# Differential attention: the scores of a head as three products over 64 rows, its two halves in turn

## The chip, the cores and the metric

One core of one Trainium2 chip. The metric is device microseconds of one launch; lower is better. The core has five engines with instruction streams of their own: PE (TensorE, the matrix products), DVE (VectorE), ACT (ScalarE), POOL (GpSimd) and SP (SyncE, which here only issues DMA transfers). They wait for each other by semaphores. Matrix products read SBUF and write PSUM; DVE and ACT read the products from PSUM.

## What is computed

Two hybrid layers (an RWKV mixer, a short convolution and differential attention side by side, then an output projection), with an attention layer, two feed-forward layers and a recurrent layer around and behind them. The change is in differential attention. A head has width 128, made of two halves of 64; each half has a softmax of its own, and the second is subtracted from the first:

```
q_l, k_l = rope(heads(q)), rope(heads(k))            # heads: (token, head, half j of 2, 64)
s    = einsum('bqhjd,bkhjd->bhjqk', q, k) * 64**-0.5
p    = softmax(s)
attn = p[:, :, 0] - lam * p[:, :, 1]
o    = einsum('bhqk,bkhe->bqhe', attn, v)
o    = rms_norm(o) * (1 - lam_init) * silu(z)
```

There are 512 tokens of the sequence and 256 of a context. Layer 0 has 4 heads and six query blocks of 128: blocks 0 to 3 look at all 768 keys, blocks 4 and 5 at 256. Layer 1 has 4 heads and four query blocks, all against 768 keys.

## The kernel before

Operands are kept in two parts, high and low (type fp32r), and a product is the sum hi·hi + hi·lo + lo·hi. The q and k of each head lie split in DRAM, 128 rows (two halves of 64) by tokens.

`attn_phase` runs an order written out by hand for PE, DVE and ACT; each executes its instructions in the order of the program. POOL and SP are placed by a scheduler. The loop goes over the units of all heads, where a unit is one head and one query block (24 in layer 0, 16 in layer 1). Iteration i issues, in this order:

- `scores(i, 0)`, `scores(i, 1)`: for each half j, matrix products into a PSUM tile `s` (tag `s2`, two buffers of 128x1024, one for each half). Then for that half DVE takes the row maximum (`mx`, L1177), and ACT the exponential with its sum (`p`, L1179).
- finishing work of a head, where one is due (transposes at L1251, product with the gate; the reciprocal root).
- `combine(i-1)` on DVE: `rc` (L1189, L1190) and `A = p0 + rc*p1` (L1192).
- `transpose(i-2)`: A is turned by PE in blocks of 128 (L1204) into the tile `ax`; ACT casts the high part `ath` (L1207) and DVE subtracts for the low part `atl` (L1208).
- `values(i-3)`, for every second unit: attn by v on PE (L1219), evicted twice by ACT (`osq`, `osb`).
- one step of a modulation stream that belongs to the next stages (layer 0 in every iteration, layer 1 in every second): a weight is loaded, split by ACT (`whi`, L295) and POOL (`wlo`, L298), and multiplied on PE (L817, L818); now and then L837 puts a finished row into `ax`.

`load(h)` brings the operands of a head: that of head 0 ahead of the loop, the others when the second unit of the head before is built. The stacked form is what the first matrix product of a key range needs: `qs[j]` holds q's high part of half j in 64 rows and its low part in the other 64; `kd[j]` holds k's high part of half j twice. So L1173 makes hi·hi + lo·hi in one product over 128 rows, and L1174 adds hi·lo over 64 rows from `kl`. Key ranges are columns 0 to 512 and 512 to 768 of `s`.

In the later attention layer ("attn2"), a pair of heads has the same three products over 64 rows already, from unstacked operands (L1842); the first head's three are issued ahead of the second's.

Of the kernel before, what the change touches and what calls it, by code (L numbers as in the profile page):

```python
# [19 lines left out]
P = 128  # L20
# [20 lines left out]
T = TL + TC  # L41
# [172 lines left out]
class Kern:  # L214
# [881 lines left out]
    def attn_phase(self, l, es):  # L1096
        nc = self.nc
        self.wpool = WP[1]
        last = l == DEPTH - 1
        D_ = self.D_  # L1100
# [9 lines left out]
        n = TL if last else T  # L1110
        with ExitStack() as e2:
            p2 = self.pool("ps2", space=PSUM, es=e2)
            pa = self.pool("paa", space=PSUM, es=e2)
            self.pm, self.nmm = pa, 1
            ap = self.pool("at", es=e2)
# [14 lines left out]
            nc.vector.tensor_scalar(out=sg, in0=self.pc(f"subln{l}"), scalar1=0.5 * (1.0 - lam0), scalar2=None, op0=ALU.mult)  # L1130
            def load(h):


                H = dict(h=h)
                lo64, hi64 = slice(0, 64), slice(64, P)
                (qh, ql), (kh, kl) = D_[f"q{h}"], D_[f"k{h}"]
                H["kl"] = self.t(ap, [P, T], "kl", 2, F32R)
                H["qs"], H["kd"] = [], []
                for j, r in enumerate((lo64, hi64)):
                    a, b = self.t(ap, [P, T], f"qs{j}", 2, F32R), self.t(ap, [P, T], f"kd{j}", 2, F32R)  # L1140
                    for i, o in enumerate((lo64, hi64)):
                        nc.sync.dma_start(out=a[o, 0:n].bitcast(F32), in_=(qh, ql)[i ^ j][r, 0:n])
                        nc.sync.dma_start(out=b[o, :].bitcast(F32), in_=kh[r, :])
                    H["qs"].append(a)
                    H["kd"].append(b)
                nc.sync.dma_start(out=H["kl"].bitcast(F32), in_=kl)
                H["v"] = self.t(ap, [P, 6, 128], "vhi", 2, F32R), self.t(ap, [P, 6, 128], "vlo", 2, F32R)
                for i, v in enumerate(H["v"]):
                    nc.sync.dma_start(out=v.bitcast(F32), in_=D_["v"][i][:, :, h * 128:h * 128 + 128].rearrange("b p c -> p b c"))
                H["z"] = self.t(ap, [P, T], "z", 2)  # L1150
                nc.sync.dma_start(out=H["z"][:, 0:n], in_=D_[f"z{h}"][:, 0:n])
                H["osb"], H["osq"] = self.t(ap, [P, T], "osb", 2), self.t(ap, [P, T], "osq", 1)
                H["mx"], H["sm"] = self.t(ap, [P, 6, 2], "mx", 2), self.t(ap, [P, 6, 2], "sm", 2)
                for c, nm in {0: ((2, "yc0"), (3, "yc1")), 1: ((0, "yr0"), (1, "yr1"))}.get(h, ()):
                    for i in range(2):
                        nc.sync.dma_start(out=self.yh[c][i][:, 0:n].bitcast(F32), in_=D_[nm][i][:, 0:n])
                return H
# [1 line left out]

            first = lambda qp: 0 if qp < 2 else 512  # L1160

            def scores(u, j):

                H, qp, qi = u["H"], u["qp"], u["qi"]
                k0 = first(qp)
                nk = T - k0
                q = slice(qp * 256 + qi * 128, qp * 256 + qi * 128 + 128)
                r = slice(j * 64, j * 64 + 64)
                s = self.t(p2, [P, 1024], "s2", 2)[:, 0:nk]
                qs, kd = H["qs"][j], H["kd"][j]  # L1170
                for a, b in ((0, min(nk, 512)), (512, nk)):
                    if b > a:
                        nc.tensor.matmul(s[:, a:b], lhsT=qs[:, q], rhs=kd[:, k0 + a:k0 + b], start=True, stop=False)  # L1173
                        nc.tensor.matmul(s[:, a:b], lhsT=qs[r, q], rhs=H["kl"][r, k0 + a:k0 + b], start=False, stop=True)  # L1174
                c = qp * 2 + qi
                mx, sm = (H[x][:, c, j:j + 1] for x in ("mx", "sm"))
                nc.vector.tensor_reduce(out=mx, in_=s, axis=AX.X, op=ALU.max, negate=True)  # L1177
                e = self.t(ap, [P, T], f"p{j}", 2)
                nc.scalar.activation(e[:, 0:nk], s, AF.Exp, bias=mx, accum_out=sm)  # L1179
                u["p"].append(e[:, 0:nk])  # L1180

            def combine(u):

# [50 lines left out]
            def gains(p_):  # L1234

                H, a, b = (p_[x] for x in "Hab")
                cols = self.rsqrt_step(*p_["rs"])
                nb = (b - a) // P
                p_["dg"] = self.t(ap, [P, 6, P], "dg", 1)
                e1, e2 = (nc.vector if p_["quick"] else nc.gpsimd for i in range(2))  # L1240
                e1.tensor_copy(out=p_["dg"][:, 0:nb, :], in_=cols.unsqueeze(2).broadcast_to([P, nb, P]))
                e2.tensor_tensor(out=H["osb"][:, a:b], in0=H["osb"][:, a:b], in1=H["z"][:, a:b], op=ALU.mult)

            def finish(p_):
                H, t0, t1 = (p_[x] for x in "Hab")
# [13 lines left out]
            with tc_manual(self.tc, MS):  # L1259
                heads = [load(0)]  # L1260
                us, due, parts = [], {}, {}
                at = lambda i: us[i] if 0 <= i < N else None
                for i in range(N + 7):
                    if i < N:
                        h, c = divmod(i, nq)
                        if c == 1 and h < 3:
                            heads.append(load(h + 1))
                        us.append(dict(H=heads[h], qp=c // 2, qi=c % 2, p=[], last=c == nq - 1))
                    u, a, t, v = at(i), at(i - 1), at(i - 2), at(i - 3)
                    for j in range(2):  # L1270
                        if u:
                            scores(u, j)
                    if i - 2 in due:
                        finish(parts[i - 2])
                    if i - 1 in due:
                        gains(parts[i - 1])
                    if a:
                        combine(a)
                    for j in range(2):
                        if t:  # L1280
                            transpose(t, 4 * j)
                    if v and v["qi"]:
# [427 lines left out]
    def attn2(self):  # L1710


        nc = self.nc
# [6 lines left out]
        ap = self.pool("a2", es=e2)  # L1720
        hi, lo = self.h
# [93 lines left out]
        hs = (slice(0, 64), slice(64, 128))  # L1815
# [19 lines left out]

        def scores(u):
            (qh, ql), (kh, kl) = get(QK, (0, u["hp"]), 2)
            u["ps"] = []
            for h in hs:
                ps = self.t(self.pm, [P, 512], "z0", 2)  # L1840
                for i, (x, y) in enumerate(((qh, kh), (qh, kl), (ql, kh))):
                    nc.tensor.matmul(ps[:, 0:u["nk"]], lhsT=x[h, u["q"]], rhs=y[h, 0:u["nk"]], start=i == 0, stop=i == 2)  # L1842
                u["ps"].append(ps)

        def soft(u):
            u["s"] = []
# [87 lines left out]
        def get(table, key, n):  # L1934
            while len(table.get(key, ())) < n:
                fill(1)
            return table[key]
# [22 lines left out]
        with tc_manual(self.tc, SM):  # L1960
            us = []
            fill(CF[3])
            bias = {0: biases(0)}
            P_ = {}
            for i in range(18):
                u = None
                if i < 16:
# [3 lines left out]
                    u = dict(hp=hp, qb=qb, nk=(qb + 1) * 128, q=slice(qb * 128, qb * 128 + 128), bias=bias[hp], p=P_[hp])  # L1971
# [16 lines left out]
                if i == 6:  # L1988
# [7 lines left out]
                    t = self.t(a3, [P, 128], "tr")  # L1996
# [206 lines left out]
```

## Time and profile before

| | |
|---|---|
| runs | 2801.47, 2799.72, 2792.19 us; median 2799.72 |
| profiled execution | 2795.74 us, of which the span of the core is 2794.0 |
| busy over the span | PE 90%, PEld (weight loads) 74%, DVE 55%, ACT 37%, POOL 27% |
| mean granted clock of TensorE | 0.938 |
| layer 0's attention loop | 585.8 to 742 us of the span, and the last units behind it |
| layer 1's attention loop | 1305.9 to about 1418 us |

PE's busy time is modelled from pipelined instructions, so the distance between two starts (the pitch) says more than a duration. The granted clock is 1.00 at 2.4 GHz and 0.50 at 1.2 GHz. Two rows that print alike and overlap stand as one row with x2.

### The profile page before, as it was taken

What the parts mean: (1) busy time and instruction counts of PE and PEld (TensorE: products, weight loads), DVE (VectorE), ACT (ScalarE), POOL (GpSimd) and SP (SyncE); (2) the same over time, 40 slices, a digit from 0 to 9 for tenths busy, and PEclk for the clock granted to TensorE, in tenths of its full rate; (3) what the DMA queues carried; (4) which work ended last, traced back from release to release, by engine and by line L of the source; (5) the groups of instructions that cost most, each with busy time, mean ns of one, the idle gap of its engine ahead of it and who ended that gap; (6) DMA issues with size and microseconds to landing.
All of it is one profiled execution on the core that took longest, in us unless ns stands there. A gap on an engine that the chain in (4) does not pass through costs nothing.

```text
span 2794.0 us, 42466 instructions
## 1 busy us (share of the span) xinstructions
PE 2522.0 (90%) x16698; PEld 2074.8 (74%) x16698; DVE 1530.4 (55%) x2949; ACT 1030.2 (37%) x1946; POOL 743.1 (27%) x635
## 2 busy tenths in 40 slices
PE   4989998979888989998988998899999987999997
PEld 2767776845687766766668877788888876988886
DVE  7266665236644477643756666564432676644423
ACT  4232222235534322322554456543222455433221
POOL 2311113314453222221223245331101353411101
PEclk8999999978899998998899999999999998999999
DMA  5332334475331333336531211212233222232232
GB/s 209 116 111 72 84 91 148 140 208 153 123 104 59 124 97 101 93 103 202 160 106 42 72 54 38 76 61 91 94 91 97 73 68 77 77 104 91 91 96 77
DMA packets 174935, 284.85 MB, mean 102 GB/s; under 512 B 53776, under 2 KB 110992, under 8 KB 174736
## 3 DMA queue, kind: packets, MB, share of 16 engines
q1 hardware_dynamic: 174736, 282.15, 32.6%
q8 instruction: 131, 2.15, 0.3%
q14 instruction: 68, 0.56, 0.1%
HBM read 235.68 MB, written 46.40 MB: 101 GB/s over the span
## 4 chain that ended last, share of the span: by engine, by line
PE 35%; DVE 8%; ACT 5%; DMA 2%; POOL 2%; issue 2%; SPq 0%; POOLq 0%; ACTq 0%; DVEq 0%
PE mm L1483 6%; PE mm L1481 6%; PE mm L1484 6%; PE mm L1520 5%; PE mm L322 4%; PE mm L1587 2%; PE s L1174 1%; ACT whi L295 1%; PE s L1173 1%; PE z L1823 1%; DMA wraw<-in_fg_dram 1%; DVE wl L304 1%; DVE wlo L298 1%; DVE w L1859 1%; PE po L1219 1%
## 5 line engine op out<-in xcount | busy, mean ns | idle before, releaser
L295 ACT CAST whi<-wraw 128x1024 fp32r<-128x1024 f32 (+2 forms) x311 | 318.0, 1026 | 648.2 <-PE mm L1483 281.9
L298 POOL TENSOR_TENSOR wlo<-wraw,whi 128x1024 fp32r<-128x1024 f32 (+1 forms) x122 | 291.4, 2391 | 703.7 <-ACT whi L295 675.3
L1483 PEld LDWEIGHTS mm<-hlo,whi 128*128 128x128 f32 x1632 | 311.4, 191 | 74.0
L322 PE MATMUL mm<-hhi,whi 128*128 128x512 f32 (+1 forms) x992 | 330.0, 364 | 17.1 <-DVE sz L925 6.0
L1481 PE MATMUL mm<-hhi,whi 128*128 128x512 f32 x816 | 329.1, 403 | 9.5 <-ACT whi L295 9.3
L1483 PE MATMUL mm<-hlo,whi 128*128 128x256 f32 x1632 | 332.2, 286 | 0.0
L1484 PE MATMUL mm<-hhi,wlo 128*128 128x512 f32 x816 | 325.7, 400 | 6.4 <-POOL wlo L298 6.4
L298 DVE TENSOR_TENSOR wlo<-wraw,whi 128x1024 fp32r<-128x1024 f32 (+1 forms) x189 | 234.4, 1244 | 175.8 <-ACT whi L295 172.9
L322 PE MATMUL mm<-hlo,whi 128*128 128x512 f32 (+1 forms) x992 | 321.8, 360 | 0.2 <-POOL hlo L863 0.2
L322 PE MATMUL mm<-hhi,wlo 128*128 128x512 f32 (+1 forms) x992 | 319.2, 358 | 0.0
L322 PEld LDWEIGHTS mm<-hhi,whi 128*128 128x128 f32 x992 | 186.3, 201 | 49.0 <-DVE sz L925 6.9
L322 PEld LDWEIGHTS mm<-hlo,whi 128*128 128x128 f32 x992 | 183.7, 201 | 23.9 <-issue 3.6
L322 PEld LDWEIGHTS mm<-hhi,wlo 128*128 128x128 f32 x992 | 182.9, 201 | 24.3 <-issue 2.1
L1481 PEld LDWEIGHTS mm<-hhi,whi 128*128 128x128 f32 x816 | 155.3, 190 | 14.5 <-ACT whi L295 11.5
L1484 PEld LDWEIGHTS mm<-hhi,wlo 128*128 128x128 f32 x816 | 158.6, 195 | 7.5 <-POOL wlo L298 7.5
L2054 POOL TENSOR_TENSOR g<-g,rsb 128x512 f32<-128x512 f32 x44 | 57.5, 1307 | 397.4 <-DVE g L2053 397.4
L1177 DVE TENSOR_REDUCE mx<-s 128x1 f32<-128x768 f32 (+1 forms) x80 | 67.4, 849 | 78.7 <-PE s L1174 78.3
L1520 PE MATMUL mm<-yhi,whi 128*128 128x256 f32 (+1 forms) x280 | 93.3, 335 | 12.4 <-ACT whi L295 10.5
L1549 POOL TENSOR_TENSOR acc<-acc,sq 128x256 f32<-128x256 f32 x48 | 51.2, 1071 | 195.1 <-ACT sq L1547 195.1
L1179 ACT ACTIVATE p<-s,mx 128x768 f32<-128x768 f32 (+1 forms) x80 | 65.1, 815 | 102.3 <-DVE mx L1177 88.3
L2056 DVE SCALAR_TENSOR_TENSOR th<-mm,g 128x512 f32<-128x512 f32 x44 | 30.4, 690 | 115.7 <-PE mm L1484 108.8
L1520 PE MATMUL mm<-yhi,wlo 128*128 128x256 f32 (+1 forms) x280 | 91.6, 328 | 0.0
(432 smaller groups left out, 5797.0 us busy)
## 6 DMA issues: line engine op xcount, KB each, us to landing
wraw<-in_win_dram SPq DMA_DIRECT2D x76, 512.0 KB, 3.6
wraw<-in_modw_dram SPq DMA_DIRECT2D x48, 512.0 KB, 4.5
wraw<-in_fg_dram SPq DMA_DIRECT2D x44, 512.0 KB, 3.3
wraw<-in_fu_dram SPq DMA_DIRECT2D x44, 512.0 KB, 3.3
wraw<-in_fd_dram SPq DMA_DIRECT2D x32, 512.0 KB, 3.5
wraw<-in_wout_dram SPq DMA_DIRECT2D x24, 512.0 KB, 3.4
wraw<-in_wv_dram SPq DMA_DIRECT2D x16, 512.0 KB, 3.4
wraw<-in_rgin_dram SPq DMA_DIRECT2D x16, 512.0 KB, 3.4
```

The costliest lines, as they stand in the source:

```text
L295: nc.scalar.copy(out=hi, in_=raw)
L298: (nc.gpsimd if pool else nc.vector).tensor_tensor(out=lo, in0=raw, in1=hi.bitcast(F32), op=ALU.subtract)
L322: mm = nc.tensor.matmul(pp, lhsT=w[:, k, :], rhs=mv(kc)[sel], start=(kc == 0 and w is hi and sel == 0), stop=(kc == tot - 1 and w is lo))
L1177: nc.vector.tensor_reduce(out=mx, in_=s, axis=AX.X, op=ALU.max, negate=True)
L1179: nc.scalar.activation(e[:, 0:nk], s, AF.Exp, bias=mx, accum_out=sm)
L1481: self.nc.tensor.matmul(ps, lhsT=w[0][:, kc, :], rhs=hi[:, kc, :], start=kc == 0, stop=False)
L1483: self.nc.tensor.matmul(ps[:, q], lhsT=w[0][:, kc, :], rhs=lo[i][kc], start=False, stop=False)
L1484: self.nc.tensor.matmul(ps, lhsT=w[1][:, kc, :], rhs=hi[:, kc, :], start=False, stop=kc == KC - 1)
L1520: self.nc.tensor.matmul(p_, lhsT=a[:, k, :], rhs=mov(kc, s)[b], start=kc == 0 and i == 0, stop=kc == n - 1 and i == 2)
L1549: nc.gpsimd.tensor_tensor(out=acc[:, q], in0=acc[:, q], in1=sq, op=ALU.add)
L1587: nc.tensor.matmul(p_[:, s], lhsT=a[:, kc, :], rhs=b(kc), start=kc == 0 and i == 0, stop=kc == 7 and i == 2)
L2054: nc.gpsimd.tensor_tensor(out=g, in0=g, in1=self.rsb, op=ALU.mult)
```

## The change

Three edits:

1. `load(h)`: eight half-tile transfers into the stacked `qs0, kd0, qs1, kd1` and one full tile `kl` become four full-tile transfers, `qhi, qlo, khi, klo`. Nothing is stored twice.
2. `scores(u)`: per key range and half, one product over 128 rows and one over 64 become three over 64 rows. Half 0 uses rows 0 to 63, half 1 rows 64 to 127, and the two alternate. Both `s2` buffers are taken before the first product, and all twelve products stand ahead of either maximum. Maxima and exponentials follow as before.
3. attn2's `scores`: the same six products, alternating between the two heads where they stood head by head; both PSUM buffers are taken first.

```diff
             def load(h):
...
-                H["kl"] = self.t(ap, [P, T], "kl", 2, F32R)
-                H["qs"], H["kd"] = [], []
-                for j, r in enumerate((lo64, hi64)):
-                    a, b = self.t(ap, [P, T], f"qs{j}", 2, F32R), self.t(ap, [P, T], f"kd{j}", 2, F32R)
-                    for i, o in enumerate((lo64, hi64)):
-                        nc.sync.dma_start(out=a[o, 0:n].bitcast(F32), in_=(qh, ql)[i ^ j][r, 0:n])
-                        nc.sync.dma_start(out=b[o, :].bitcast(F32), in_=kh[r, :])
-                    H["qs"].append(a)
-                    H["kd"].append(b)
-                nc.sync.dma_start(out=H["kl"].bitcast(F32), in_=kl)
+                for nm, m in (("q", n), ("k", T)):
+                    H[nm] = [self.t(ap, [P, T], nm + x, 2, F32R) for x in ("hi", "lo")]
+                    for s, t in zip(D_[f"{nm}{h}"], H[nm]):
+                        nc.sync.dma_start(out=t[:, 0:m].bitcast(F32), in_=s[:, 0:m])
...
-            def scores(u, j):
+            def scores(u):
...
-                s = self.t(p2, [P, 1024], "s2", 2)[:, 0:nk]
-                qs, kd = H["qs"][j], H["kd"][j]
+                (qh, ql), (kh, kl) = H["q"], H["k"]
+                ss = [self.t(p2, [P, 1024], "s2", 2)[:, 0:nk] for _ in range(2)]
                 for a, b in ((0, min(nk, 512)), (512, nk)):
                     if b > a:
-                        nc.tensor.matmul(s[:, a:b], lhsT=qs[:, q], rhs=kd[:, k0 + a:k0 + b], start=True, stop=False)
-                        nc.tensor.matmul(s[:, a:b], lhsT=qs[r, q], rhs=H["kl"][r, k0 + a:k0 + b], start=False, stop=True)
+                        for i, (x, y) in enumerate(((qh, kh), (qh, kl), (ql, kh))):
+                            for j, s in enumerate(ss):
+                                r = slice(j * 64, j * 64 + 64)
+                                nc.tensor.matmul(s[:, a:b], lhsT=x[r, q], rhs=y[r, k0 + a:k0 + b], start=i == 0, stop=i == 2)
...
-                    for j in range(2):
-                        if u:
-                            scores(u, j)
+                    if u:
+                        scores(u)
...
-            for h in hs:
-                ps = self.t(self.pm, [P, 512], "z0", 2)
-                for i, (x, y) in enumerate(((qh, kh), (qh, kl), (ql, kh))):
+            u["ps"] = [self.t(self.pm, [P, 512], "z0", 2) for _ in hs]
+            for i, (x, y) in enumerate(((qh, kh), (qh, kl), (ql, kh))):
+                for h, ps in zip(hs, u["ps"]):
                     nc.tensor.matmul(ps[:, 0:u["nk"]], lhsT=x[h, u["q"]], rhs=y[h, 0:u["nk"]], start=i == 0, stop=i == 2)
```

On PE, the fourth unit of layer 0's first head stood so before (numbers behind a name are buffers; a wait in brackets is for the engine that last read the buffer, here ACT's exponential):

```order
L1173 MATMUL s_959_5616<-kd_907_5467,qs_906_5466 128x512 [waits Activation_49]
L1174 MATMUL s_959_5616<-kl_5465,qs_906_5466 128x512
L1173 MATMUL s_959_5616<-kd_907_5467,qs_906_5466 128x256
L1174 MATMUL s_959_5616<-kl_5465,qs_906_5466 128x256
L1173 MATMUL s_961_5624<-kd_909_5473,qs_908_5472 128x512 [waits Activation_49]
L1174 MATMUL s_961_5624<-kl_5465,qs_908_5472 128x512
L1173 MATMUL s_961_5624<-kd_909_5473,qs_908_5472 128x256
L1174 MATMUL s_961_5624<-kl_5465,qs_908_5472 128x256
```

The same unit on PE in the changed kernel:

```order
L1166 MATMUL s_957_5616<-khi_5469,qhi_5465 128x512 [waits Activation_49]
L1166 MATMUL s_958_5617<-khi_5469,qhi_5465 128x512 [waits Activation_49]
L1166 MATMUL s_957_5616<-klo_5470,qhi_5465 128x512
L1166 MATMUL s_958_5617<-klo_5470,qhi_5465 128x512
L1166 MATMUL s_957_5616<-khi_5469,qlo_5466 128x512
L1166 MATMUL s_958_5617<-khi_5469,qlo_5466 128x512
L1166 MATMUL s_957_5616<-khi_5469,qhi_5465 128x256
L1166 MATMUL s_958_5617<-khi_5469,qhi_5465 128x256
L1166 MATMUL s_957_5616<-klo_5470,qhi_5465 128x256
L1166 MATMUL s_958_5617<-klo_5470,qhi_5465 128x256
L1166 MATMUL s_957_5616<-khi_5469,qlo_5466 128x256
L1166 MATMUL s_958_5617<-khi_5469,qlo_5466 128x256
```

Eight products became twelve; the wait for the second buffer moved from the fifth product to the second, ahead of almost all of half 0's work.

On SP, the transfers of layer 0's first head before:

```order
L1142 DMA qs_906_5466<-q0h_85 64x768
L1143 DMA kd_907_5467<-k0h_93 64x768
L1142 DMA qs_906_5466<-q0l_86 64x768
L1143 DMA kd_907_5467<-k0h_93 64x768
L1142 DMA qs_908_5472<-q0l_86 64x768
L1143 DMA kd_909_5473<-k0h_93 64x768
L1142 DMA qs_908_5472<-q0h_85 64x768
L1143 DMA kd_909_5473<-k0h_93 64x768
L1146 DMA kl_5465<-k0l_94 128x768
L1149 DMA vhi_5479<-vh_101 128x6x128
```

And in the changed kernel:

```order
L1137 DMA qhi_5465<-q0h_85 128x768
L1137 DMA qlo_5466<-q0l_86 128x768
L1137 DMA khi_5469<-k0h_93 128x768
L1137 DMA klo_5470<-k0l_94 128x768
L1140 DMA vhi_5473<-vh_101 128x6x128
```

k's low part is the fourth transfer of a head where it was the ninth, and everything behind it on SP's queue is five transfers nearer.

On PE in attn2, the six products of one unit before:

```order
L1842 MATMUL z_2706_14527<-qk1hi_14387,qk0hi_14381 128x384 [waits DVE_49]
L1842 MATMUL z_2706_14527<-qk1lo_14388,qk0hi_14381 128x384
L1842 MATMUL z_2706_14527<-qk1hi_14387,qk0lo_14382 128x384
L1842 MATMUL z_2707_14531<-qk1hi_14387,qk0hi_14381 128x384 [waits DVE_49]
L1842 MATMUL z_2707_14531<-qk1lo_14388,qk0hi_14381 128x384
L1842 MATMUL z_2707_14531<-qk1hi_14387,qk0lo_14382 128x384
```

And the same unit in the changed kernel:

```order
L1834 MATMUL z_2698_14623<-qk1hi_14483,qk0hi_14477 128x384 [waits DVE_49]
L1834 MATMUL z_2699_14624<-qk1hi_14483,qk0hi_14477 128x384 [waits DVE_49]
L1834 MATMUL z_2698_14623<-qk1lo_14484,qk0hi_14477 128x384
L1834 MATMUL z_2699_14624<-qk1lo_14484,qk0hi_14477 128x384
L1834 MATMUL z_2698_14623<-qk1hi_14483,qk0lo_14478 128x384
L1834 MATMUL z_2699_14624<-qk1hi_14483,qk0lo_14478 128x384
```

Only the order changed, and with it the place of the second buffer's wait.

## Rows read from the trace of the kernel before

**Rows 1.** Windows, one per unit of layer 0's second head: length, busy time (count), clock, DMA.

```profile
621.09:628.36 7.27, 7.27 (x42) 5.07 (x40) 4.66 (x9) 3.29 (x7) 1.77 (x2) 1.00 1.03 282
628.36:632.41 4.05, 4.05 (x15) 1.99 (x14) 2.51 (x6) 3.38 (x9) 2.87 (x2) 1.00 1.05 282
632.41:637.61 5.20, 5.20 (x25) 3.13 (x24) 5.09 (x8) 4.34 (x9) 3.15 (x2) 1.00 0.29 114
637.61:643.37 5.76, 5.76 (x31) 3.70 (x30) 5.27 (x8) 4.86 (x11) 4.14 (x2) 1.00 0.74 222
643.37:654.69 11.32, 7.77 (x41) 5.83 (x40) 8.06 (x16) 5.05 (x14) 5.52 (x3) 0.79 0.42 142
654.69:660.93 6.24, 5.81 (x22) 3.74 (x20) 3.27 (x9) 3.16 (x8) 1.12 (x1) 0.56 0.90 235
```

**Rows 2.** Windows of layer 1: same columns (PE, PEld, DVE, ACT, POOL, clock, DMA).

```profile
1326.44:1380.30 53.86, 51.00 (x236) 32.73 (x234) 43.57 (x72) 34.36 (x74) 14.17 (x8) 0.91 0.61 181
1380.30:1394.00 13.70, 13.24 (x44) 9.46 (x45) 6.12 (x15) 4.08 (x9) 2.97 (x2) 0.50 0.39 126
```

**Rows 3.** Timeline of PE, one unit against 768 keys: start, duration, line.

```profile
628.36 0.40 PE L1173 MATMUL s<-kd,qs 128*128 128x512 f32 x1
...
631.22 0.44 PE L1204 MATMUL ax<-con,A 128*128 128x128 f32 x2
```

**Rows 4.** Timeline of PE, first products of two units at half clock.

```profile
594.80 0.79 PE L1173 MATMUL s<-kd,qs 128*128 128x512 f32 x1
...
599.74 0.79 PE L1173 MATMUL s<-kd,qs 128*128 128x512 f32 x1
```

**Rows 5.** Timeline of PE, attn2: six products of 512 columns and the next.

```profile
1544.34 0.50 PE L1842 MATMUL z<-qk1hi,qk0hi 64*128 64x512 f32 x2
1544.68 0.40 PE L1842 MATMUL z<-qk1lo,qk0hi 64*128 64x512 f32 x2
1544.91 0.40 PE L1842 MATMUL z<-qk1hi,qk0lo 64*128 64x512 f32 x2
1545.24 0.50 PE L1481 MATMUL mm<-hhi,whi 128*128 128x512 f32 x1
```

**Rows 6.** Timeline of PE, attn2: six products of 256 columns and the next.

```profile
1559.79 0.40 PE L1842 MATMUL z<-qk1hi,qk0hi 64*128 64x256 f32 x2
...
1560.35 0.38 PE L1785 MATMUL mm<-whi,hhi 128*128 128x256 f32 x1
```

**Rows 7.** Timeline of DVE and ACT: both maxima of a unit, and its second exponential.

```profile
634.50 1.83 DVE L1177 TENSOR_REDUCE mx<-s 128x1 f32<-128x768 f32 x2
...
636.43 0.89 ACT L1179 ACTIVATE p<-s,mx 128x768 f32<-128x768 f32 x1
```

**Rows 8.** Timeline of PE, first products of both layers; idle before and its releaser.

```profile
585.82 0.77 PE L1173 MATMUL s<-kd,qs 128*128 128x512 f32 x1 [9.75 <-DMA kd<-k0h]
590.60 0.79 PE L1174 MATMUL s<-kl,qs 64*128 64x512 f32 x1 [4.01 <-DMA kl<-k0l]
...
1311.17 0.79 PE L1174 MATMUL s<-kl,qs 64*128 64x512 f32 x1 [4.51 <-DMA kl<-k0l]
```

**Rows 9.** Timeline of SP's queue, the eighth and ninth transfer: issue, duration.

```profile
582.27 0.45 SPq L1143 DMA_DIRECT2D kd<-k0h  x1
583.18 0.33 SPq L1146 DMA_DIRECT2D kl<-k0l  x1
```

**Rows 10.** DMA view of 582.2 to 583.3: size, us from issue to landing.

```profile
kl<-k0l SPq DMA_DIRECT2D x1, 384.0 KB, 7.4
kd<-k0h SPq DMA_DIRECT2D x1, 192.0 KB, 7.4
```

**Rows 11.** Timeline of DVE, POOL and PE around a stall of layer 0.

```profile
647.45 3.13 DVE L1192 SCALAR_TENSOR_TENSOR A<-p,rc,p 128x768 f32<-128x768 f32 x1
...
651.23 1.01 PE L837 MATMUL ax<-con,wraw 4*128 4x2 f32 x4 [3.37 <-DVE atl L1208]
```

**Rows 12.** Timeline of PE, layer 1: a wait of PE.

```profile
1380.76 0.58 PE L837 MATMUL ax<-con,wraw 4*128 4x2 f32 x2 [1.74 <-DVE atl L1208]
```

More of the change, by code (lines that the diff above doesn't have):

```diff
@@ L1134, in load @@
                 H = dict(h=h)
-                lo64, hi64 = slice(0, 64), slice(64, P)
-                (qh, ql), (kh, kl) = D_[f"q{h}"], D_[f"k{h}"]
-                H["kl"] = self.t(ap, [P, T], "kl", 2, F32R)
-                H["qs"], H["kd"] = [], []
-                for j, r in enumerate((lo64, hi64)):
-                    a, b = self.t(ap, [P, T], f"qs{j}", 2, F32R), self.t(ap, [P, T], f"kd{j}", 2, F32R)
-                    for i, o in enumerate((lo64, hi64)):
-                        nc.sync.dma_start(out=a[o, 0:n].bitcast(F32), in_=(qh, ql)[i ^ j][r, 0:n])
-                        nc.sync.dma_start(out=b[o, :].bitcast(F32), in_=kh[r, :])
-                    H["qs"].append(a)
-                    H["kd"].append(b)
-                nc.sync.dma_start(out=H["kl"].bitcast(F32), in_=kl)
+                for nm, m in (("q", n), ("k", T)):
+                    H[nm] = [self.t(ap, [P, T], nm + x, 2, F32R) for x in ("hi", "lo")]
+                    for s, t in zip(D_[f"{nm}{h}"], H[nm]):
+                        nc.sync.dma_start(out=t[:, 0:m].bitcast(F32), in_=s[:, 0:m])
                 H["v"] = self.t(ap, [P, 6, 128], "vhi", 2, F32R), self.t(ap, [P, 6, 128], "vlo", 2, F32R)
@@ L1167, in scores @@
                 q = slice(qp * 256 + qi * 128, qp * 256 + qi * 128 + 128)
-                r = slice(j * 64, j * 64 + 64)
-                s = self.t(p2, [P, 1024], "s2", 2)[:, 0:nk]
-                qs, kd = H["qs"][j], H["kd"][j]
+                (qh, ql), (kh, kl) = H["q"], H["k"]
+                ss = [self.t(p2, [P, 1024], "s2", 2)[:, 0:nk] for _ in range(2)]
                 for a, b in ((0, min(nk, 512)), (512, nk)):
                     if b > a:
-                        nc.tensor.matmul(s[:, a:b], lhsT=qs[:, q], rhs=kd[:, k0 + a:k0 + b], start=True, stop=False)
-                        nc.tensor.matmul(s[:, a:b], lhsT=qs[r, q], rhs=H["kl"][r, k0 + a:k0 + b], start=False, stop=True)
+                        for i, (x, y) in enumerate(((qh, kh), (qh, kl), (ql, kh))):
+                            for j, s in enumerate(ss):
+                                r = slice(j * 64, j * 64 + 64)
+                                nc.tensor.matmul(s[:, a:b], lhsT=x[r, q], rhs=y[r, k0 + a:k0 + b], start=i == 0, stop=i == 2)
                 c = qp * 2 + qi
[L1176 to L1180, printed above, removed]
+                for j, s in enumerate(ss):
+                    mx, sm = (H[x][:, c, j:j + 1] for x in ("mx", "sm"))
+                    nc.vector.tensor_reduce(out=mx, in_=s, axis=AX.X, op=ALU.max, negate=True)
+                    e = self.t(ap, [P, T], f"p{j}", 2)
+                    nc.scalar.activation(e[:, 0:nk], s, AF.Exp, bias=mx, accum_out=sm)
+                    u["p"].append(e[:, 0:nk])
             def combine(u):
@@ L1837, in scores @@
             (qh, ql), (kh, kl) = get(QK, (0, u["hp"]), 2)
-            u["ps"] = []
-            for h in hs:
-                ps = self.t(self.pm, [P, 512], "z0", 2)
-                for i, (x, y) in enumerate(((qh, kh), (qh, kl), (ql, kh))):
+            u["ps"] = [self.t(self.pm, [P, 512], "z0", 2) for _ in hs]
+            for i, (x, y) in enumerate(((qh, kh), (qh, kl), (ql, kh))):
+                for h, ps in zip(hs, u["ps"]):
                     nc.tensor.matmul(ps[:, 0:u["nk"]], lhsT=x[h, u["q"]], rhs=y[h, 0:u["nk"]], start=i == 0, stop=i == 2)
-                u["ps"].append(ps)
         def soft(u):
```

## The prediction

> **What bounds the kernel now.** I read the windows first. In layer 0's second head, whose six units take 39.84 us, PE is busy for all of the first four units and for 35.86 us of the whole [rows 1]; in layer 1 for 51.00 of 53.86 us [rows 2]. So PE sets the pace in attention, except in the fifth unit, where it is busy for 7.77 of 11.32 us. But DVE is not far behind: it is busy for 5.09 of the 5.20 us of the third unit, 5.27 of 5.76 of the fourth, 28.9 of the 39.84 us of the head, and 43.57 of 53.86 us in layer 1.
>
> Then the timeline of PE. A unit against 768 keys takes 2.86 us for its eight products, from the first one's start to the start of the next work [rows 3], and 4.94 us at half clock [rows 4]. At the start of each layer's loop PE waits for k's low part: in layer 0 the first product starts at 585.82, the second only at 590.60, in layer 1 the second at 1311.17 after a wait of 4.51 [rows 8].
>
> Last the timeline of DVE and ACT: after the scores come two maxima, 1.83 us in all, and the second exponential, 0.89, which starts at 636.43, 0.10 after the maxima end [rows 7]. From the first maximum's start to that exponential's end it is 636.43 + 0.89 - 634.50 = 2.82 us. The scores' tiles are free then.
>
> **The products.** No row shows twelve products over 64 rows with ranges of 512 and 256 columns in one unit, but attn2 has both halves of it. Six of 512 columns take 1545.24 - 1544.34 = 0.90 us until the next work starts [rows 5], six of 256 take 1560.35 - 1559.79 = 0.56 [rows 6]. The rows come in pairs (x2 in one row), so products in rows 0 to 63 and in rows 64 to 127 run beside each other: three steps for six products. The two ranges of a unit need 0.90 + 0.56 = 1.46 us at most, less if the entry to the second range costs nothing extra: its steps without the entry are half of the first range's, (1544.91 - 1544.68) / 2 x 3 = 0.35, so 0.90 + 0.35 = 1.25. I take 1.3: PE saves 1.56 us in a 768-key unit. In a 256-key unit the same six products before are four; I estimate half of 2.86 less the 512 columns, about 1.2, against 0.56: 0.6 saved. At half clock I double 1.3 to 2.6, against 4.94.
>
> The Trainium skill ("TensorE: Matmul & The Clock Gate", Part 3, The mechanism) says that products start and end strictly in program order. In attn2 before, all three of the first head are queued ahead of the second head's, and yet rows of 1544.34 show the two heads' first products together; this trace does not agree. By that rule the third edit would save three steps in each of attn2's units: 3 x 0.23 us with 512 columns, 3 x 0.12 with 256, between these with 384 and about 0.33 with 128, four units of each, some 7.6 us. By the rows they overlap already, and it saves nothing.
>
> So I cost **attn2's reorder** at nothing. Its bounds: a second buffer that is awaited earlier can hold up the first head for the 0.2 to 2 us of a late buffer in a few units, 0 to +3 us; a gain below 1 us.
>
> **How much of it shortens a unit.** After the change the next unit's first two products wait for both exponentials of the unit before, and both halves end together. So a 768-key unit is at least 1.3 + 0.1 + 2.82 = 4.2 us long, whatever PE has to do otherwise. DVE's own load is the other floor: 17.53 us over the four 768-key units of rows 1 (4.66 + 2.51 + 5.09 + 5.27), 4.4 each, of which nothing goes away. So I take periods of 4.4 to 4.7, or 1.3 + the old unit's remainder, whichever is longer [rows 1]:
> - 7.27: remainder 4.41, new 5.7, saves 1.6.
> - 4.05: below the floor; new 4.4, loses 0.35.
> - 5.20: new 4.7, saves 0.5.
> - 5.76: new 4.7 (remainder 2.9 + 1.3 = 4.2), saves 1.1.
> - 11.32 and 6.24: 256 keys; 0.6 at most each. The first holds a DVE instruction of 3.13 us and a PE wait of 3.37 [rows 11], which the change leaves alone; I take 0.7 for both.
>
> That is 3.5 us a head, for three heads 10.5. Of the first head the units behind the cold start remain: 2.0. Layer 0's steady part: **-12.5** (bounds: all of PE's saving, 4 x 1.56 + 1.2 = 7.4 a head and -25 in all, to -4 if DVE's stalls take most of it).
>
> Layer 1: the first window has about 9.6 units in 53.86 us, 5.6 each. At DVE's 43.57 / 9.6 = 4.5 plus 0.2, they come to 4.7: -8.7. Of the rest, two units are at half clock [rows 2], where 2.3 each are to be had, but PE also waits there; I take -2.5. Together **-11** (bounds -24 by PE alone, -5).
>
> **The starts.** In layer 0 the ninth transfer, k's low part, is issued at 583.18 and lands 7.4 later, 590.58; the eighth, half its size, is issued at 582.27 and lands 7.4 later too [rows 9, 10]. So a full tile lands 0.9 us behind the transfer before it, and a half tile takes no less: the first four landed by 585.82, the other five by 590.58, 0.95 each. Four full tiles then land by about 585.8. The other bound is by bytes: 1152 KB in those 4.76 us, and the first four would carry 768 KB more, 3.2 us: 589.0. I take 585.9, because the row of the full tile shows no longer time than the half one's.
>
> From there: before, unit 1 starts at 594.80, unit 2 at 599.74 [rows 4], and its scores end 4.94 later, 604.7. After, all at half clock: unit 0's scores 585.9 to 588.5, then 2.9 of maxima and exponentials, unit 1 591.4 to 594.0, unit 2 596.9 to 599.5. That is 5.2 earlier; with steps that stand closer at half clock, up to 7. I take -6, and the same for layer 1, whose wait is 4.51: **-12** for both (bounds -4, when landings go by bytes, and -14). The 40 transfers that fall away (five for each of eight heads) bring everything behind them on SP's queue forward, the modulation weights too; that hides no wait I could price, and it costs nothing.
>
> **Sum.** -12.5 - 11 - 12 = -35.5 us. Against the profiled execution, 2795.74, that is 2760.2. The median of the runs shown, 2799.72, is 4.0 above that execution, and the time asked for is a median; I stand in the middle, at **2762 us**. What a measurement can tell from no change is taken as 0.3%, 8.4 us.
>
> **Rivals.**
> - **A, PE alone sets it**: every microsecond that PE saves shows, -25 - 24 - 14 = -63, about 2735. Against it: DVE's 5.09 of 5.20 and the 4.2 us from the scores to free buffers. Chance 0.08.
> - **B, evacuation takes it all back**: maxima, exponentials, `rc`, `A` and `atl` keep the pace of before, and only the starts gain: -12 to -15, about 2784. For it: DVE's 43.57 of 53.86 us, and the unit of 4.05 that gets longer. Against it: DVE idles a quarter of each head. It decides where 4.7 is really 5.4. The Trainium skill ("TensorEngine Tiling (Array Packing)", PSUM Bottleneck) speaks for this one: packing products speeds up TensorE and not the evacuation of PSUM. Chance 0.18.
> - **C, the clock falls** (the other side). In a unit with little else to do (4.05 - 2.86 = 1.2 us of it) PE would now wait for 4.2 - 1.3 - 1.2 = 1.7 us. In layer 1 a wait of 1.74 us [rows 12] stands at the head of a window whose granted clock is 0.50 for 13.7 us [rows 2], and behind the wait of 3.37 [rows 11] comes a unit at 0.56 [rows 1]. At half clock throughout, the 22 us of other PE work of a head (35.86 less 4 x 2.86 + 2 x 1.2) would be about 16 longer and its scores as long as before (4 x 2.6 + 2 x 1.2 = 12.8 against 13.8): 55 us for 39.84, +15 a head. It turns the sum positive once more than a third of the units are cold; with half of them cold +30 - 12 = +18, about 2815. Against it: such waits stand between short units only, and the four units of 621 to 643 run at 1.00 with DVE as busy as it will be. Chance 0.12, of which 0.08 end above +8.4.
> - **D, the halves don't run beside each other** when they alternate: twelve products in a row, 2.3 us, and 2.9 behind them make units of 5.2. The short unit loses 1.2, the long ones gain 0.5, the cold starts lose what the loads gain: about 2797. Against it stand the pairs of rows 5 and 6. Chance 0.05.
> - **E, attn2's reorder pays** by the rule in program order: the forecast and 7 us more, 2755, within the range. Chance 0.02.
>
> **How the numbers follow.** The forecast (-15 to -50) has 0.55. Faster by more than 0.3%: forecast, A, E, most of B: 0.80. Within 0.3%: a fifth of B, some of C, D: 0.12. Slower: 0.08. The range reaches to A on one side, and over B on the other, 2736 to 2789; it leaves out D, C and half of A. The likeliest case's own range is 2748 to 2785.
>
> **What would show it.** Twelve products of a unit start in six pairs and end in about 1.3 us; if singly, D. Units of 4.05 become 4.4 and those of 5.76 about 4.7; DVE busy for nearly all of a 768-key unit, and PE waiting for ACT's exponential ahead of scores. The second product of each layer follows the first without a wait for k's low part. Windows of the heads keep a granted clock of 0.8 or more; below 0.7, C. In attn2 the starts of pairs are as before. The forecast fails if PE's wait for the exponential is followed by half clock, or if `A` and `rc` stall longer beside POOL now that units follow more closely.

## The result, and the profile after

The changed kernel takes 2761.49 us (median of 2758.36 to 2762.74), the kernel before 2800.59 in the same comparison: ratio 0.9865, interval 0.9845 to 0.9885, 39 us less. The forecast was 2762.

Page of the changed kernel, its head: span, then busy time, share and instructions of the engines.

```profile
span 2756.6 us, 42685 instructions
...
PE 2467.2 (90%) x16842; PEld 2057.8 (75%) x16842; DVE 1529.0 (55%) x2949; ACT 1028.1 (37%) x1946; POOL 742.8 (27%) x635
```

To see where 37.4 us of span went, the program needs marks. DVE runs the same 2949 instructions in both kernels, so I measure each layer's loop from `sg` (L1130, ahead of it) to the last product with the gate (L1252 before, L1245 after). The view of L1130 in the changed kernel (first and last start stand in the row):

```profile
L1130 DVE TENSOR_SCALAR sg<-par x2: 146/146/147, 572.2 to 1275.8; 128x1 f32<-128x1 f32 x2
```

Times in us of the span, and lengths; "all else" is the span without the two loops:

| us | layer 0: loop | to its fourth unit | layer 1: loop | to its fourth unit | all else |
|---|---|---|---|---|---|
| before | 575.3 to 754.0, 178.7 | 607.72, 32.4 | 1299.3 to 1428.8, 129.5 | 1326.44, 27.1 | 2485.8 |
| changed | 572.2 to 729.8, 157.6 | 598.00, 25.8 | 1275.8 to 1389.8, 114.0 | 1297.63, 21.8 | 2485.0 |
| difference | -21.1 | -6.6 | -15.5 | -5.3 | -0.8 |

So the loops lost 36.6 us: 11.9 at the two starts (the first three units), 24.7 in the rest. All that is not attention is as long as before; that the loop begins 3.1 us earlier is spread of one execution, which goes both ways in the runs below (571.5 to 580.3 for the same program).

Windows of the changed kernel, layer 0's second head by units, as [rows 1]:

```profile
609.91:616.48 6.57, 5.85 (x45) 4.72 (x44) 4.82 (x9) 3.18 (x7) 1.70 (x2) 1.00 0.98 362
616.48:620.72 4.24, 3.12 (x20) 1.72 (x19) 2.56 (x6) 3.73 (x9) 3.04 (x2) 1.00 0.82 225
620.72:625.27 4.55, 4.17 (x28) 2.85 (x28) 4.46 (x7) 3.35 (x7) 3.27 (x2) 1.00 0.11 44
625.27:630.14 4.87, 4.75 (x35) 3.44 (x35) 4.77 (x7) 4.72 (x12) 2.82 (x2) 1.00 0.58 163
630.14:641.69 11.55, 8.12 (x44) 6.84 (x43) 9.71 (x17) 5.98 (x16) 5.85 (x4) 0.70 0.49 171
641.69:646.63 4.94, 4.51 (x24) 3.11 (x24) 3.21 (x9) 3.08 (x8) 2.21 (x2) 0.65 0.86 274
```

PE is no longer busy throughout the first four units, and DVE (third pair) is, in the third and fourth. The head went from 39.84 to 36.72 us; the fifth unit did not shrink.

Timeline of PE in the changed kernel, the fourth head's second unit, and the start of its third:

```profile
686.05 0.50 PE L1166 MATMUL s<-khi,qhi 64*128 64x512 f32 x2
686.39 0.39 PE L1166 MATMUL s<-klo,qhi 64*128 64x512 f32 x2
686.62 0.40 PE L1166 MATMUL s<-khi,qlo 64*128 64x512 f32 x2
686.86 0.28 PE L1166 MATMUL s<-khi,qhi 64*128 64x256 f32 x2
686.97 0.27 PE L1166 MATMUL s<-klo,qhi 64*128 64x256 f32 x2
687.09 0.28 PE L1166 MATMUL s<-khi,qlo 64*128 64x256 f32 x2
687.30 0.44 PE L1197 MATMUL ax<-con,A 128*128 128x128 f32 x2
...
689.50 0.49 PE L1166 MATMUL s<-khi,qhi 64*128 64x512 f32 x1 [0.84 <-ACT p L1172]
```

Twelve products in six pairs, 1.25 us for the 2.86 of [rows 3]; then PE waits for an exponential, where it was busy throughout such a unit before [rows 1]. What that wait holds back is seen 35 us earlier in the same timeline:

```profile
654.76 0.49 PE L1166 MATMUL s<-khi,qhi 64*128 64x512 f32 x1 [0.85 <-ACT p L1172]
655.64 0.49 PE L1166 MATMUL s<-khi,qhi 64*128 64x512 f32 x1 [0.39 <-ACT p L1172]
655.64 0.72 PE L1166 MATMUL s<-klo,qhi 64*128 64x512 f32 x2
```

Half 0's first product starts when the first exponential is done, half 1's when the second is, 0.88 later; half 0's second product stands behind it in the queue and waits with it.

Timeline of PE, the starts of both layers, as [rows 8]:

```profile
581.82 0.80 PE L1166 MATMUL s<-khi,qhi 64*128 64x512 f32 x2 [8.87 <-DMA khi<-k0h]
582.80 0.80 PE L1166 MATMUL s<-klo,qhi 64*128 64x512 f32 x2 [0.18 <-DMA klo<-k0l]
...
1283.13 0.79 PE L1166 MATMUL s<-khi,qhi 64*128 64x512 f32 x2 [6.83 <-DVE sz L304]
```

The wait of 4.01 us for k's low part is 0.18, that of 4.51 is gone. In layer 1 the first product itself now starts with the end of a DVE instruction (`sz`), and not with a landing.

### The profile page after: what moved, and what is told of

Read it like the earlier page. It is cut to its first block, busy times and chain, and to the rows that moved or that the text cites. A ratio compares the mean times of both kernels' runs of the same rounds, so it can differ in the third digit from the quotient of the medians.

```text
span 2756.6 us, 42685 instructions
## 1 busy us (share of the span) xinstructions
PE 2467.2 (90%) x16842; PEld 2057.8 (75%) x16842; DVE 1529.0 (55%) x2949; ACT 1028.1 (37%) x1946; POOL 742.8 (27%) x635
## 4 chain that ended last, share of the span: by engine, by line
PE 35%; DVE 9%; ACT 5%; POOL 2%; issue 2%; DMA 1%; POOLq 0%; SPq 0%; ACTq 0%; DVEq 0%
PE mm L1512 7%; PE mm L1475 6%; PE mm L1473 6%; PE mm L1476 6%; PE mm L322 4%; PE mm L1579 2%; PE z L1815 1%; ACT whi L295 1%; DVE wl L304 1%; DVE mx L1170 1%; PE s L1166 1%; DMA vl<-sz 1%; DVE xc L2090 1%; DVE w L1850 1%; DVE hlo L1614 1%
## 5 line engine op out<-in xcount | busy, mean ns | idle before, releaser
L1473 PEld LDWEIGHTS mm<-hhi,whi 128*128 128x128 f32 x816 | 156.0, 191 | 14.5 <-ACT whi L295 11.6
L1512 PE MATMUL mm<-yhi,whi 128*128 128x256 f32 (+1 forms) x280 | 93.4, 335 | 12.5 <-ACT whi L295 10.6
L1512 PE MATMUL mm<-ylo,whi 128*128 128x256 f32 (+1 forms) x280 | 91.8, 328 | 0.0
```

What stands on the lines that cost most here:

```text
L1473: self.nc.tensor.matmul(ps, lhsT=w[0][:, kc, :], rhs=hi[:, kc, :], start=kc == 0, stop=False)
L1512: self.nc.tensor.matmul(p_, lhsT=a[:, k, :], rhs=mov(kc, s)[b], start=kc == 0 and i == 0, stop=kc == n - 1 and i == 2)
```

## Experiments

All were timed against the kernel before in the same way. "Layer 0" and "layer 1" are the loops of one profiled execution, by the marks above; e1, whose attention is that of before, shows that they spread by 2 to 4 us.

| kernel | ratio | interval | us | layer 0 | layer 1 |
|---|---|---|---|---|---|
| changed | 0.9865 | 0.9845 to 0.9885 | 2761.49 | 157.6 | 114.0 |
| e1 attn2 alone | 0.9996 | 0.9975 to 1.0017 | 2797.35 | 180.9 | 133.3 |
| e2 nine transfers | 0.9890 | 0.9865 to 0.9916 | 2768.40 | 165.5 | 113.2 |
| e3 half by half | 0.9884 | 0.9857 to 0.9912 | 2765.05 | 165.4 | 116.9 |
| e4 stacked, grouped | 0.9875 | 0.9848 to 0.9901 | 2764.47 | 165.8 | 114.6 |
| e5 before, no maxima | 0.9943 | 0.9920 to 0.9966 | 2788.46 | 170.8 | 128.7 |
| e6 changed, no maxima | 0.9755 | 0.9725 to 0.9784 | 2730.19 | 146.8 | 96.0 |
| e7 wlo on DVE | 0.9966 | 0.9949 to 0.9983 | 2790.11 | 184.1 | 118.5 |
| e8 three and three | 0.9850 | 0.9823 to 0.9876 | 2757.85 | 157.8 | 115.7 |
| e9 stream early | 0.9902 | 0.9878 to 0.9925 | 2770.61 | 171.6 | 112.6 |
| e10 put early | 0.9833 | 0.9810 to 0.9857 | 2755.30 | 155.5 | 113.1 |
| e11 e10, no maxima | 0.9719 | 0.9695 to 0.9742 | 2723.98 | 147.7 | 91.4 |
| e12 half grouped | 0.9908 | 0.9885 to 0.9931 | 2775.24 | 171.5 | 118.3 |

**e1, attn2's order alone.** The last hunk of the diff, on the kernel before.

> The kernel before with the third edit alone: attn2's six products alternate, attention is as before. My theory (the two heads' products overlap already in the old order): no change, 2800 us within 3. Rival (products run in program order, so alternating saves three steps in each of sixteen units): 7.6 us less, about 2793. Also: before attention starts, the first 570 us are the same program as before, so any shift of DVE's instructions there tells how much of the 4 us that the changed kernel was early by then comes with the change.

No change, and the rival's 7.6 us (ratio 0.9973) lie just outside the interval. In the changed kernel attn2's pairs start as in [rows 5]. Its timeline:

```profile
1562.63 0.50 PE L1834 MATMUL z<-qk1hi,qk0hi 64*128 64x512 f32 x2
1562.97 0.40 PE L1834 MATMUL z<-qk1lo,qk0hi 64*128 64x512 f32 x2
1563.20 0.40 PE L1834 MATMUL z<-qk1hi,qk0lo 64*128 64x512 f32 x2
```

**e2, the transfers.**

```diff
...
+                xk = self.t(ap, [P, T], "xk", 2, F32R)
+                for j, r in enumerate((slice(0, 64), slice(64, P))):
+                    for i in range(2):
+                        nc.sync.dma_start(out=H["q"][i ^ j][r, 0:n].bitcast(F32), in_=(qh, ql)[i ^ j][r, 0:n])
+                        nc.sync.dma_start(out=(H["k"][0], xk)[i][r, :].bitcast(F32), in_=kh[r, :])
+                nc.sync.dma_start(out=H["k"][1].bitcast(F32), in_=kl)
```

> The changed kernel with a head's transfers as before: eight half tiles (two of them a second copy of k's high part, into a tile that nothing reads) and k's low part as the ninth. Products as changed. My theory (the starts of both layers gain some 10 to 12 us from four transfers in place of nine, the products the rest): about 2772, 9 to 12 us over the changed kernel. Rival one (transfers are hidden anyway, all comes from the products): 2761. Rival two (the gain is the transfers'): 2795 or more.

By the ratios, 31 of 38 us of the gain remain with nine transfers, which puts rival two out. The four give 7, by the difference of two ratios whose intervals touch, so the time alone does not put rival one out. The trace does: from `sg` to the fourth unit it takes 30.9 us in layer 0 (577.8 to 608.6) and 25.9 in layer 1 (1289.0 to 1314.9), against 25.8 and 21.8 in the changed kernel. That is 9.2, within the 9 to 12 expected, and more than these starts spread: the five other kernels with four transfers and with maxima (e3, e7 to e10) need 24.9 to 25.7 and 21.3 to 22.4. Of the 11.9 us at the starts the products are left with 2.7.

**e4 and e12, the stacked operands in another order.** The products of before, first the 128-row ones of both halves, then the 64-row ones (e4); or the same within each half (e12). The products in e4's edit:

```diff
...
+                for j, s in enumerate(ss):
+                    for a, b in cols:
+                        nc.tensor.matmul(s[:, a:b], lhsT=H["qs"][j][:, q], rhs=H["kd"][j][:, k0 + a:k0 + b], start=True, stop=False)
+                for a, b in cols:
+                    for j, s in enumerate(ss):
+                        r = slice(j * 64, j * 64 + 64)
+                        nc.tensor.matmul(s[:, a:b], lhsT=H["qs"][j][r, q], rhs=H["kl"][r, k0 + a:k0 + b], start=False, stop=True)
...
```

> The kernel before (stacked operands, nine transfers, attn2 as before) with a unit's eight products put in another order: the four over 128 rows of both halves, then the four over 64 rows, alternating. Theory: each change between 128 and 64 rows costs about 0.2 us, and before there were eight in a unit, now two; the same columns stream as in the changed kernel (1536 over 128 rows and 768 in pairs against 2304 in pairs), so a unit's products take 1.4 to 1.5 us and the steady gain comes without unstacking, about 2779. Rival (it is the unstacked operands and rows in halves that do it; a product over 128 rows keeps its step of 0.43 and 0.31): 2.0 us a unit, about 2789. If the order is worth nothing: 2800.

> The kernel before with each half's four products in the order two over 128 rows, then two over 64 rows; nothing else. Theory (what cost PE before was each change between 128 and 64 rows, 0.2 us): four changes in a unit for eight, so 2.86 - 0.8 = 2.06 us for a unit's products, and the steady part gains half to two thirds of what the stacked-grouped kernel gains: about 2782. Rival (the gain of that kernel came from putting both halves' products together, not from the changes of rows): 2.7 us or more a unit, 2797 or more.

Timeline of PE in e4, one unit of 768 keys (rows of 512 and 256 columns that overlap stand as one):

```profile
698.07 0.85 PE L1172 MATMUL s<-kd,qs 128*128 128x512 f32 x4
698.85 0.62 PE L1176 MATMUL s<-kl,qs 64*128 64x512 f32 x4
699.39 0.44 PE L1207 MATMUL ax<-con,A 128*128 128x128 f32 x2
```

And in e12, the same unit:

```profile
700.75 0.51 PE L1173 MATMUL s<-kd,qs 128*128 128x512 f32 x2
701.20 0.62 PE L1175 MATMUL s<-kl,qs 64*128 64x512 f32 x2
701.74 0.61 PE L1173 MATMUL s<-kd,qs 128*128 128x512 f32 x2
702.29 0.62 PE L1175 MATMUL s<-kl,qs 64*128 64x512 f32 x2
702.84 0.33 PE L1205 MATMUL ax<-con,A 128*128 128x128 f32 x1
```

The same eight products take 2.86 us with eight changes between 128 and 64 rows, 702.84 - 700.75 = 2.09 with four (2.07 in most units; 2.06 was expected), and 699.39 - 698.07 = 1.32 with two (in a unit that waits for no exponential), where the 64-row ones also pair. So a change of rows costs 0.2 us, and that is what the unit lost. Unstacking is one way to be rid of the changes, not the reason: e4, stacked and with nine transfers, is as fast as the changed kernel within the intervals, 15 us better than I expected of it; e12 is 7 us better than expected.

Where the 0.2 us go, the weight loads (PEld) show. Timelines of PE and PEld before, the first half of the unit of [rows 3]:

```profile
628.36 0.40 PE L1173 MATMUL s<-kd,qs 128*128 128x512 f32 x1
628.68 0.50 PE L1174 MATMUL s<-kl,qs 64*128 64x512 f32 x1
629.11 0.38 PE L1173 MATMUL s<-kd,qs 128*128 128x256 f32 x1
...
628.68 0.18 PEld L1174 LDWEIGHTS s<-kl,qs 64*128 64x128 f32 x1 [0.36 <-issue]
629.11 0.19 PEld L1173 LDWEIGHTS s<-kd,qs 128*128 128x128 f32 x1 [0.25 <-issue]
```

And of PEld in the changed kernel, the second and third pair of the unit shown above, whose products start at 686.39 and 686.62:

```profile
686.16 0.19 PEld L1166 LDWEIGHTS s<-klo,qhi 64*128 64x128 f32 x2
686.39 0.19 PEld L1166 LDWEIGHTS s<-khi,qlo 64*128 64x128 f32 x2
```

In the changed kernel each of these loads starts 0.23 us ahead of its product, under the product before it. Before, behind a change of rows, it starts together with its product, and its 0.18 to 0.19 us are not hidden. In the kernel before this is so for all 196 products in and right behind the scores that follow a change of rows at full clock (load and product start within 3 ns), and for none of the 26 that follow none. This is read from the traces; no run changes the loads alone. One rival is that a product waits because it adds to the columns that the one before it has just written. It falls with e3's rows below: three such products in a row start 0.34 (the first stands behind a change of rows) and 0.23 us apart.

**e3 and e8, the order of the halves.** The changed kernel, six products of half 0 ahead of six of half 1 (e3), or three and three in each key range (e8). The edit of e8:

```diff
-                        for i, (x, y) in enumerate(((qh, kh), (qh, kl), (ql, kh))):
-                            for j, s in enumerate(ss):
-                                r = slice(j * 64, j * 64 + 64)
+                        for j, s in enumerate(ss):
+                            r = slice(j * 64, j * 64 + 64)
+                            for i, (x, y) in enumerate(((qh, kh), (qh, kl), (ql, kh))):
```

> The changed kernel with the six products of half 0 queued ahead of the six of half 1, as attn2 had them before. My theory (the two row halves run beside each other whatever the queue's order is, and only a wait holds back what is queued behind it): half 0 now starts as soon as the first exponential is done, 0.9 us ahead of the second, so its maximum comes earlier in units that wait for the exponentials: 0 to 10 us less than the changed kernel, about 2756. Rival (alternating is what makes halves overlap): twelve products in a row, 2.3 us for 1.3, about 2785.

> The changed kernel with the products of a key range queued as three of half 0, then three of half 1 (as attn2 had them), instead of alternating. Theory (a product can start beside one that stands up to three places ahead in the queue, as attn2's rows and the half-by-half kernel show, but not six): halves overlap fully, 1.25 us a unit as in the changed kernel, and half 0's first three no longer stand behind the wait for the second exponential: 2755 to 2763. Rival (any order but alternating loses part of the overlap): 1.8 us a unit, about 2767.

Timeline of PE in e3, a unit that waits for nothing (half 0's first three products, then half 1's first):

```profile
663.84 0.50 PE L1166 MATMUL s<-khi,qhi 64*128 64x512 f32 x1
664.18 0.39 PE L1166 MATMUL s<-klo,qhi 64*128 64x512 f32 x1
664.41 0.39 PE L1166 MATMUL s<-khi,qlo 64*128 64x512 f32 x1
664.41 0.50 PE L1166 MATMUL s<-khi,qhi 64*128 64x512 f32 x2
...
665.67 0.44 PE L1197 MATMUL ax<-con,A 128*128 128x128 f32 x2
```

Half 1, six places behind, starts 0.57 us late, and the unit takes 1.83 us. Neither side of e3's expectation held: the order matters, but by half, and e3's time is not told from the changed kernel's. With three places (e8) units without a wait take 1.25 us in six pairs, as with alternation, and the time is not told from the changed kernel's. Timeline of PE in e8:

```profile
686.54 0.51 PE L1166 MATMUL s<-khi,qhi 64*128 64x512 f32 x2
...
687.79 0.44 PE L1197 MATMUL ax<-con,A 128*128 128x128 f32 x2
```

**e5 and e6, the row maxima left out** in the kernel before and in the changed one. The softmax is the same as long as no exponential overflows.

```diff
...
-                    nc.vector.tensor_reduce(out=mx, in_=s, axis=AX.X, op=ALU.max, negate=True)
-                    nc.scalar.activation(e[:, 0:nk], s, AF.Exp, bias=mx, accum_out=sm)
+                    nc.scalar.activation(e[:, 0:nk], s, AF.Exp, accum_out=sm)
```

> The kernel before without the row maxima of differential attention: the exponentials take the scores as they are, which gives the same softmax while nothing overflows. DVE loses 80 instructions, 67 us busy. My theory (PE set the pace before): little, 0 to 8 us less than before, about 2795. Rival (the evacuation bounded already before): 20 us less or more.

> The changed kernel without the row maxima, as the one beside it. My theory (after the change a 768-key unit is bounded by maxima and exponentials, 4.2 us from scores to scores, and by DVE's 4.4): it gains more from this than the kernel before does, 10 to 20 us less than the changed kernel, about 2748; ACT's own 4.3 us a unit in layer 0 is the next bound. Rival (PE still sets the pace after the change): the same 0 to 8 us as for the kernel before, about 2757.

By the ratios, the kernel before gains 0.57%, 16 us; the changed one 0.9865 - 0.9755 = 1.1%, 31 us. Evacuation bounds more of the loop after the change than before it, as argued, and both numbers are larger than expected. Before, the gain sits in the units in which PE waits for `atl`, and behind them: the long one of the second head falls from 11.32 to 9.64, the third of the third head from 8.75 to 7.09 and the one behind it, at a granted clock of 0.54 before, from 9.65 to 5.75, while the second head's units of 4.05 and 5.76 stay.

**e7, the modulation's low parts on DVE.** `WP = (1,0,...)` for `(1,1,...)`.

> The changed kernel with the low parts of the modulation weights made by DVE in the attention loops (1.24 us each) and not by POOL (2.4 us each). Theory (a DVE instruction that starts beside POOL's stretches to the end of it, and this sets the long fifth unit of each head): A takes 1.02 and rc 0.22 everywhere, the 256-key unit of 11.5 us falls to about 8, but each unit against 768 keys has 1.24 us more on a DVE that is full: 2755 to 2770. Rival (the long unit has another cause, such as L837's own chain): it stays above 10, and the time rises by 15 us or more.

DVE in layer 0, grouped by line, in the changed kernel (count, busy, mean ns):

```profile
L1185 DVE SCALAR_TENSOR_TENSOR A<-p,rc,p 128x768 f32<-128x768 f32 x16 | 22.7, 1416 | 0.6
L1183 DVE SCALAR_TENSOR_TENSOR rc<-rc,nlam,sm 128x1 f32<-128x1 f32 x24 | 19.6, 816 | 0.9
```

And in e7, with the low parts among them:

```profile
L298 DVE TENSOR_TENSOR wlo<-wraw,whi 128x1024 fp32r<-128x1024 f32 x24 | 31.0, 1293 | 25.2 <-ACT whi L295 25.2
...
L1185 DVE SCALAR_TENSOR_TENSOR A<-p,rc,p 128x768 f32<-128x768 f32 x16 | 17.2, 1075 | 0.6
...
L1183 DVE SCALAR_TENSOR_TENSOR rc<-rc,nlam,sm 128x1 f32<-128x1 f32 x24 | 5.8, 244 | 0.9
```

`A` and `rc` do shrink when POOL is quiet (19 us together), but DVE waits 25.2 us for ACT's high parts in their place, and the kernel is 29 us slower than the changed one. The long unit stays at 13.2 us, with `A` at 1.02 in it and PE still waiting 2.94 us ahead of L837: POOL's stall is not the only thing that can make it long. How much of it that stall made in the changed kernel e7 can't tell, since in this same unit DVE now waits 1.93 us for a high part and spends 1.23 on the low part.

**e9, e10, e11, L837's place.** e9 moves the modulation stream's step to just behind the scores; e10 moves only the put (L837, L838) of that step; e11 is e10 without maxima. All stand on e8. The edit of e9, in the loop:

```diff
                     if u:
                         scores(u)
+                    if l == 0 or i % 2:
+                        next(mods, None)
...
```

> The three-and-three kernel with each step of the modulation stream moved from the end of an iteration to just behind the scores, ahead of the transposes. Theory (the long units of a head come from L837, which takes a buffer of ax that waits for atl, and atl stands on DVE behind two maxima, rc and A; the wait of 3 us stayed when POOL's stall was taken away): L837 now finds a free ax buffer, the units of 9 to 11.6 us fall to 6 or 7, and the half clock behind them goes: 2742 to 2752. Rival (the wait only moves to the transposes, which need both ax buffers): no gain, 2755 to 2765.

> As the kernel beside it, but only the step's L837 and L838 are moved ahead of the transposes; the stream's products (L817, L818) and its next load stay at the iteration's end. Same theory: 2742 to 2752, and equal to the one beside it if L837's place is all of it. Rival: 2755 to 2765.

> The put-early kernel without the row maxima (the softmax is the same while no exponential overflows). If L837's wait and the maxima are two costs that add: 2715 to 2725. If both are the same cost, DVE's queue ahead of atl: the gain of the no-max kernel alone, about 2730.

e9 is slower than e8: the next weight's cast now stands on ACT ahead of `ath`, and when the weight is late PE waits through ACT and DVE. Timelines of ACT and PE in e9, the first unit of the second head:

```profile
616.09 1.04 ACT L295 CAST whi<-wraw 128x1024 fp32r<-128x1024 f32 x1 [4.66 <-DMA wraw<-in_modw_dram]
...
618.40 1.43 PE L837 MATMUL ax<-con,wraw 4*128 4x2 f32 x6 [6.04 <-DVE atl L1201]
```

e10 shortens two long units (9.28 to 5.86, 9.12 to 5.57) and leaves the two of 11.6 and one of 9.2, while others grow (in layer 0 one from 5.24 to 7.46, in layer 1 one from 5.87 to 8.28); in the two of 11.6 PE now waits 3.9 and 3.8 us for ACT's copy of the row. Its 2755 is not told from e8's 2758, against an expected 2742 to 2752; it lies where the rival had it. e11 is the fastest here, 2.8% below the kernel before. Its 2724 lies in the 2715 to 2725 expected if the two costs add, but its interval overlaps that of e6, so that they add isn't shown.

## Why the prediction was right, point by point

- **The products.** 1.3 us taken, 1.25 measured in units that wait for no exponential, and some 2.1 in most that do; at half clock 2.6 taken, about 2.1 measured (1283.13 to the last row's start at 1285.00 in the same timeline, and a step). The size came from attn2's rows. Why a unit had cost 2.86 the prediction didn't say; e4 and e12 did: changes between 128 and 64 rows, 0.2 us each. It spoke of the halves running beside each other (rival D), which holds, but the two stacked products grouped give the same.
- **The starts.** -12 forecast, 11.9 measured, -6.6 and -5.3; by e2 9.2 of it is the transfers'. Full tiles land about as fast as half ones: k's low part, the fourth, delays PE by 0.18 us.
- **The steady part, layer 0.** -12.5 forecast; 21.1 - 6.6 = 14.5 measured. That the sum is near is partly luck: where 3.5 us a head were forecast, the second gained 3.1 (39.84 to 36.72), the third 6.2 (39.87 to 33.67) and the fourth with the end of the loop 3.7 (53.22 to 49.53). In the third head 4.5 of the 6.2 come from one unit (9.65 to 5.18), which had run at a granted clock of 0.54 and now ran at 0.80; nothing in the forecast stood for that. By units of the second head: 7.27 to 6.57 (5.7 expected), 4.05 to 4.24 (4.4), 5.20 to 4.55 (4.7), 5.76 to 4.87 (4.7). In the third and fourth head the short unit became 3.45, below the floor of 4.2: its floor is paid in the next unit, whose products start with the first exponential and then wait for the second (2.1 us from first to last in place of 1.25). The second and third unit together take 8.8 us in the second head and 8.0 in the fourth, against 9.25 before and 9.1 expected.
- **The steady part, layer 1.** -11 forecast, 15.5 - 5.3 = 10.2 measured, again with luck: the first window of [rows 2] holds 8.6 units and not 9.6, and its eight whole ones went from 48.1 to 43.3 us, 5.4 each and not 4.7, one of them longer (6.77 to 9.27). As much, 4.7, came from a single unit behind them, 9.88 us at a granted clock of 0.51 before and 5.15 at 0.79 after; 2.5 were forecast for all of that part.
- **The long fifth unit** kept its length (11.55), as the text said. POOL's stall of `A`, the cause it gave, is not shown to be the only one: in e7, without that stall but with more work for DVE, the wait for `atl` stayed.
- **attn2's reorder.** Nothing forecast, nothing measured; rival E is out, by time only narrowly, and the rows show the pairs in either order.
- **Rival B** (evacuation takes it back) was too strong, and its mechanism true: removing the maxima gives 31 us after the change. It was true before the change too, which the prediction's "PE sets the pace" left out: 16 us.
- **Rival C** (the clock). Heads 2, 3 and 4 of layer 0 (the last to the loop's end) ran at 0.86, 0.95 and 0.84 for 0.87, 0.83 and 0.89; the whole span at 0.94 as before. PE's waits of 0.85 us ahead of scores did not bring it down.

For the loops, starts and all, the forecast was 2.6 us too small in layer 0 and 1.5 too large in layer 1, as far as one execution can tell; that 2762 stands within a microsecond of the measurement is partly luck, since one profiled execution spreads by more.

## What to carry to other kernels

Where products over different numbers of rows alternate on PE, compare their pitch with that of equal products of the same width; if it is longer, reorder by row count first, which needs no new operands or loads. When PE's part of a loop shrinks, look for the time from its result to the freed buffer: that is the next floor, and leaving the evacuation's largest instruction out, before and after, prices it. Compare traces by marks around the stage, because the program around it shifts by several microseconds between executions.

## What the runs showed of the hardware that was not expected

- A change between products over 128 rows and over 64 costs about 0.2 us at full clock (a unit's eight products: 2.86, 2.07 and 1.32 us with eight, four and two changes; in the last the 64-row ones also pair). The weight load behind a change starts with its product, and not under the one before it.
- Products in different row halves run beside each other when they stand three places apart in the queue (e8, attn2), and start 0.57 us late when six apart (e3). A wait holds back everything behind it, of the other half too (655.64).
- A tile of half the rows takes about as long to land as a full one: 0.9 us each in [rows 9, 10], and in the changed kernel the product that needs the fourth full tile starts 0.98 us after the one that needs the third.
